# Forgetting attention: the softmax weights become the stationary operand of the weighted values

## The chip, the cores and the metric

The kernel runs on one core of a Trainium2 chip. The metric is the device time of the whole program in microseconds (us), taken over several runs; lower is better. The profile is of one execution. The engines are called as the profile calls them: PE (TensorE, matrix products), PEld (its loads of the stationary operand), DVE (VectorE), ACT (ScalarE), POOL (GpSimd) and SP, which issues most DMAs.

## What is computed

A trunk of two layers over 512 tokens of 1024 features. Layer 0 is causal softmax attention with 16 heads of 64 features and a forgetting bias; layer 1 is a gated linear recurrence (HGRN2). Each is followed by a gated MLP with a short causal convolution. The change touches only layer 0:

```python
def fox_mixer(h, w_in, b_f, w_out):
    q, k, v, fl = jnp.split(h @ w_in, [D, 2 * D, 3 * D], axis=-1)
    c = jnp.cumsum(jax.nn.log_sigmoid(fl + b_f), axis=1)
    ...
    logits = jnp.einsum('bhqd,bhkd->bhqk', qi, k) * scale
    logits = logits + (cqi[..., :, None] - c[:, :, None, :])
    logits = jnp.where(s_pos[None, :] <= t_pos[:, None], logits, -jnp.inf)
    p = jax.nn.softmax(logits, axis=-1)
    o = jnp.einsum('bhqk,bhkd->bhqd', p, v)
    ...
    return o @ w_out
```

## The kernel before

All of it lives on one core. Every float32 operand of a large product is split into two float32r parts, high and low (`split`, lines 66 to 68: ACT copies the high part, DVE subtracts to get the low one), and a product is three matmuls: high by high, high by low, low by high (`mm3`, lines 81 to 84). A projection (`proj`, line 86) makes 128 features by 512 tokens from 8 blocks of rows, 24 matmuls in all; its weights come as one 512 KB DMA into a tile `raw` (two buffers).

Attention goes over 8 pairs of heads. Four Python generators are interleaved by `conduct` (line 141): `projections` (main) issues one block of a projection, three matmuls, per step; `operands` puts finished q and k into the operands QX, KX, QQ, KK by DMA and transposes v; `maxima` computes logits to find the row maxima (tiles `mxp`); `attend` computes the logits again, transposed, with keys on the partitions (tiles `lg`), takes the exponential, masks it on POOL and splits it into `ph` and `pl`. A yield of n leaves n steps to the projections. Pair n+1's operands reuse the buffers of pair n-1, so they are begun only when pair n-1 is done. A scheduler then moves instructions within each engine; the order below is what it made.

In `attend`, one pair's transposed weights stand in five tiles: a0 (head 0, keys 0 to 127, all 512 queries), a1 (head 0, key tiles 1 and 3), c (key tile 2 of both heads), b0 and b1 (head 1). `weigh` (lines 459 to 467) uses the values as the stationary operand: 64 columns of `vh` or `vl` beside 64 columns of ones or zeros, and streams the weights of 512, 384, 256 and 128 queries past them, three matmuls per key tile. The result has features on the partitions for one head, the sum of the weights on the other 64 partitions. `evacuate` (lines 472 to 475) copies both out; the reciprocal of the sums is made with a logarithm, an exponential and a Newton step (lines 498 to 503), and `split` makes `oh` and `ol`, the operands of the output projection.

PSUM has three banks `b` for projections, three banks `s` (`side`) for all that runs beside them (mxp, rp, vT, pv), and two banks `lg`. The output projection begins before the last pairs are done: `early` (line 99) takes five blocks of output features (three in `b`, one in `s`, one in `lg`) through pairs 0 to 5, and does pairs 6 and 7 at the end. After that the MLP follows.

Of the kernel before, what the change touches and what calls it, by code (L numbers as in the profile page):

```python
# [8 lines left out]
F32 = mybir.dt.float32  # L9
# [19 lines left out]
# gain columns: att norm, hgrn norm, ffn norms, final norm, output norm, lower-bound logits  # L29
G_ATT, G_HGRN, G_FFN, G_FIN, G_ON, G_LB = 0, 1, 2, 4, 5, 6  # L30
# t-range starts of the transposed logits of key tile j
OFF = (0, 512, 1024, 896)
# [3 lines left out]
def trunk(ctx, tc, xT, gains, convs, bf, wqkv, wf, wo, wup, wdn, wh, wi, who, out):  # L36
# [8 lines left out]
    def bank(name):  # L45
        """a bank for a projection"""
        return ps.tile([P, S], F32, tag="b", name=name)

    def side(name):
        """a bank for what runs beside the projections"""  # L50
        return ps.tile([P, S], F32, tag="s", name=name)
# [34 lines left out]
    def proj(ap, xh, xl, name, kb=NB, bank=bank):  # L86
        """[128 features, S tokens] = W^T x; one step is one block of rows of W"""
# [11 lines left out]
    def early(aps, xh, xl, name, *more):  # L99
        """projections begun while the last two blocks of operands are still to come: three, and one for each  # L100
        of more, a bank and when it is free, whose weights take the place of operands used up before"""
# [39 lines left out]
    def conduct(main, *sides):  # L141
        """main issues one block of rows of a projection per step; a side stream yields how many steps
        to leave to main, or what it waits for"""
# [26 lines left out]
    class Norm:  # L170
# [24 lines left out]
        def finish(self, load=True):  # L195
            """rstd of each token, on every partition"""
# [27 lines left out]
    # =============== layer 0: forgetting attention ===============  # L224
    oscope = ExitStack()
    opool = oscope.enter_context(tc.tile_pool(name="opool", bufs=1, side="right"))
    with tc.tile_pool(name="att", bufs=2, side="right") as ap_:
# [6 lines left out]
        # first projections, block by block as x comes in  # L234
# [45 lines left out]
        # masks and persistent operands  # L280
        st = []
        for i in range(4):
            # rows of KX: k, cumulated gates, ones; of QX: q, ones, maxima; the sums of products of the low parts
            # come from KK and QQ
            t = {n: ap_.tile([P, S], F32R, name=f"{n}{i}", bufs=1) for n in ("KX", "QX", "KK", "QQ")}
            for n in ("KX", "QX"):
                G.memset(t[n][64:68].bitcast(F32), 1.0)
            st.append(t)
# [5 lines left out]
        for i in range(2):  # L294
            vh = ap_.tile([P, NT, 192], F32R, name=f"vh{i}", bufs=1)
            vl = ap_.tile([P, NT, 192], F32R, name=f"vl{i}", bufs=1)
            G.memset(vh[:, :, 64:128].bitcast(F32), 1.0)
            G.memset(vl[:, :, 64:128].bitcast(F32), 0.0)
            vst.append((vh, vl))
# [3 lines left out]
        def forget():  # L303
            """-8 * cumsum(log sigmoid) as rows, in two parts"""
# [13 lines left out]
        # pairs of heads whose keys, values, maxima and outputs are there  # L318
# [25 lines left out]
        def values(hp, o):  # L344
            """values, tokens on the partitions"""
            v32 = tmp(f"v32_{hp}")
            V.tensor_mul(v32, o, rstd)
            vh, vl = vst[hp % 2]
# [4 lines left out]
            vhv = vh.rearrange("p i (e d) -> p i e d", d=64)[:, :, 0::2, :]  # L353
            vlv = vl.rearrange("p i (e d) -> p i e d", d=64)[:, :, 0::2, :]
# [23 lines left out]
        def operands():  # L378
            """the products go on as soon as what they overwrite has been used"""
# [15 lines left out]
        def maxima():  # L395
            """of the rows of the logits; their negatives as rows of an operand"""
# [30 lines left out]
        def attend():  # L427
            """transposed logits, exponentials, weighted values with their sums beside them"""
            for hp in range(8):
# [3 lines left out]
                vh, vl = vst[hp % 2]  # L433
                parts = {}

                def logits(key, *blocks):
                    """blocks: head, key tile, first column in the bank"""
# [15 lines left out]
                    ph = ap_.tile([P, S], F32R, tag="ph", name=f"ph_{nm}", bufs=3)  # L453
                    pl = ap_.tile([P, S], F32R, tag="pl", name=f"pl_{nm}", bufs=3)
# [4 lines left out]
                def weigh(o, e, js):  # L459
                    cs = slice(64 * e, 64 * e + P)  # L460
                    for j in js:
                        ph, pl, c = parts[e, j]
                        s_ = slice(c, c + S - P * j)
                        oo = o[:, j * P:]
                        PE.matmul(oo, vh[:, j, cs], ph[:, s_], start=j == 0, stop=False)
                        PE.matmul(oo, vl[:, j, cs], ph[:, s_], start=False, stop=False)
                        PE.matmul(oo, vh[:, j, cs], pl[:, s_], start=False, stop=j == 2)

                dn = ap_.tile([P, S], F32, tag="dn", name=f"dn_{hp}", bufs=1)
                o32 = ap_.tile([P, S], F32, tag="o32", name=f"o32_{hp}", bufs=1)  # L470

                def evacuate(o, e):
                    a, b = slice(64 * e, 64 * e + 64), slice(64 - 64 * e, 128 - 64 * e)
                    A.copy(dn[a], o[b])
                    A.copy(o32[a], o[a])
# [7 lines left out]
                oa = side(f"pv_{hp}_0")  # L483
                weigh(oa, 0, (0,))
                logits("b0", (1, 0, 0))
                yield 2
                weigh(oa, 0, (1, 3))
# [3 lines left out]
                weigh(oa, 0, (2,))  # L491
                evacuate(oa, 0)
# [387 lines left out]
```

## Time and profile before

| | |
|---|---|
| median of 3 runs | 1280.43 us (1279.92 to 1281.11) |
| span of the profiled execution | 1279.4 us |
| attention with its output projection's start | 44 to 252 us of the span |
| one pair of heads in the steady part | about 26 us |
| mean granted clock of TensorE | 0.996 of full speed |

The span runs from the first to the last instruction of the profiled execution, whose own time outside the span is not listed; the median of the runs is 1.0 us above the span. In a timeline row the first number is the start, the second the duration; matmuls are pipelined, so the cost of one is the distance from its start to the next one's start, which is less than its duration. A bracket names what ended the idle time before an instruction. Line numbers are those of the kernel above.

### The profile page before, as it was taken

The numbers are of one execution on the slowest core, as the hardware profiler recorded it, in microseconds if no ns is written. First come the engines' busy times: TensorE is split into PE (matmuls) and PEld (weight loads), VectorE is DVE, ScalarE is ACT, GpSimd is POOL, SyncE is SP. The second block draws the span as 40 slices with busy tenths as digits, with TensorE's granted clock in tenths as the row PEclk, the third lists the DMA queues.
The fourth block names the chain that finished last, engine by engine and source line by source line (L and its number), as shares of the span: only waits on it lengthen the run. The fifth ranks groups of instructions, "written<-read, shape, count | busy, mean of one in ns | idle before, by whom it ended". The sixth has DMA issues, their size and how long they took to land.

```text
span 1279.4 us, 15645 instructions
## 1 busy us (share of the span) xinstructions
PE 1258.4 (98%) x5994; PEld 1042.7 (81%) x5994; DVE 803.0 (63%) x1235; ACT 589.8 (46%) x827; POOL 40.4 (3%) x110
## 2 busy tenths in 40 slices
PE   7999999999999999999999999999999999999997
PEld 5778888888888888888888888888888888888886
DVE  6767767387777777333367585566777777762233
ACT  6355556454444444222267565455544444442231
POOL 2011110000000000000100000000000000000001
PEclk9999999999999999999999999999999999999998
DMA  6544554233233333333322222222333333333321
GB/s 200 153 119 106 135 135 122 98 120 98 97 99 99 99 99 95 91 91 91 98 96 66 83 66 83 83 67 82 99 99 99 92 94 95 98 91 91 94 88 66
DMA packets 43306, 127.25 MB, mean 99 GB/s; under 512 B 5616, under 2 KB 8304, under 8 KB 43232
## 3 DMA queue, kind: packets, MB, share of 16 engines
q1 hardware_dynamic: 42592, 125.56, 32.6%
q8 instruction: 47, 0.77, 0.2%
q10 hardware_dynamic: 544, 0.52, 0.1%
q14 instruction: 27, 0.22, 0.1%
q0 software_dynamic: 96, 0.18, 0.1%
HBM read 111.43 MB, written 2.10 MB: 89 GB/s over the span
## 4 chain that ended last, share of the span: by engine, by line
PE 95%; DVE 2%; DMA 1%; ACT 1%; issue 0%; SPq 0%; POOL 0%; DVEq 0%; ACTq 0%
PE pj_up L82 12%; PE pj_up L84 12%; PE pj_up L83 12%; PE pj_dn L84 6%; PE pj_dn L82 6%; PE pj_dn L83 6%; PE i L629 1%; PE i L628 1%; PE i L626 1%; PE pj_who L83 1%; PE pj_wo L82 1%; PE pj_wo L83 1%; PE pj_who L84 1%; PE pj_who L82 1%; PE pj_wo L84 1%; PE pj_hf L82 1%
## 5 line engine op out<-in xcount | busy, mean ns | idle before, releaser
L84 PE MATMUL pj_up<-xh_f,wl_up 128*128 128x512 f32 x704 | 274.3, 390 | 0.0
L83 PE MATMUL pj_up<-xl_f,wh_up 128*128 128x512 f32 x704 | 274.3, 390 | 0.0
L82 PE MATMUL pj_up<-xh_f,wh_up 128*128 128x512 f32 x704 | 274.3, 390 | 0.0
L84 PEld LDWEIGHTS pj_up<-xh_f,wl_up 128*128 128x128 f32 x704 | 132.3, 188 | 27.5
L83 PEld LDWEIGHTS pj_up<-xl_f,wh_up 128*128 128x128 f32 x704 | 132.3, 188 | 27.3
L82 PEld LDWEIGHTS pj_up<-xh_f,wh_up 128*128 128x128 f32 x704 | 132.3, 188 | 27.2
L82 PE MATMUL pj_dn<-gh,wh_dn 128*128 128x512 f32 x330 | 131.0, 397 | 0.0
L84 PE MATMUL pj_dn<-gh,wl_dn 128*128 128x512 f32 x330 | 131.0, 397 | 0.0
L83 PE MATMUL pj_dn<-gl,wh_dn 128*128 128x512 f32 x330 | 131.0, 397 | 0.0
L67 ACT CAST wh_up<-raw_up 128x1024 fp32r<-128x1024 f32 x88 | 92.7, 1053 | 65.9 <-PE pj_up L83 51.5
L68 DVE TENSOR_TENSOR wl_up<-raw_up,wh_up 128x1024 fp32r<-128x1024 f32 x88 | 107.8, 1225 | 15.4 <-ACT wh_up L67 11.7
L68 DVE TENSOR_TENSOR wl_dn<-raw_dn,wh_dn 128x1024 fp32r<-128x1024 f32 (+1 forms) x45 | 51.1, 1136 | 97.9 <-ACT wh_dn L67 97.7
L543 DVE TENSOR_TENSOR us<-pj_up,rstd_f 128x512 f32<-128x512 f32 x88 | 60.6, 689 | 78.7 <-PE pj_up L84 78.6
L67 ACT CAST wh_dn<-raw_dn 128x1024 fp32r<-128x1024 f32 (+1 forms) x45 | 44.1, 980 | 140.4 <-PE pj_dn L83 114.0
L67 ACT CAST gh<-y 128x512 fp32r<-128x512 f32 x44 | 27.3, 620 | 115.5 <-DVE y L551 115.5
L546 ACT ACTIVATE y<-us,cv 128x512 f32<-128x512 f32 x88 | 71.7, 815 | 8.4 <-DVE us L543 7.3
L84 PEld LDWEIGHTS pj_dn<-gh,wl_dn 128*128 128x128 f32 x330 | 62.3, 189 | 15.0
L83 PEld LDWEIGHTS pj_dn<-gl,wh_dn 128*128 128x128 f32 x330 | 62.3, 189 | 15.0
L82 PEld LDWEIGHTS pj_dn<-gh,wh_dn 128*128 128x128 f32 x330 | 62.3, 189 | 15.0
L548 DVE SCALAR_TENSOR_TENSOR y<-us,cv,y 128x512 f32<-128x512 f32 x88 | 66.1, 752 | 3.0
L547 DVE SCALAR_TENSOR_TENSOR y<-us,cv,y 128x512 f32<-128x512 f32 x88 | 65.6, 745 | 0.2
L550 ACT ACTIVATE y<-y 128x512 f32<-128x512 f32 x44 | 27.8, 632 | 79.4 <-DVE y L548 79.4
(368 smaller groups left out, 2375.5 us busy)
## 6 DMA issues: line engine op xcount, KB each, us to landing
raw_up<-in_wup SPq DMA_DIRECT2D x88, 512.0 KB
raw_dn<-in_wdn SPq DMA_DIRECT2D x30, 512.0 KB
raw_dn<-in_wdn SPq DMA_DIRECT2D x15, 384.0 KB
raw_v<-in_wqkv SPq DMA_DIRECT2D x8, 512.0 KB
raw_wo<-in_wo SPq DMA_DIRECT2D x8, 512.0 KB
raw_hf<-in_wh SPq DMA_DIRECT2D x8, 512.0 KB
raw_hq<-in_wh SPq DMA_DIRECT2D x8, 512.0 KB
raw_hg<-in_wh SPq DMA_DIRECT2D x8, 512.0 KB
```

What stands on the lines that cost most here:

```text
L67: A.copy(dst_h, src)
L68: V.tensor_tensor(dst_l, src, dst_h.bitcast(F32), op=ALU.subtract)
L82: PE.matmul(o, wh_, xh_, start=first, stop=False)
L83: PE.matmul(o, wh_, xl_, start=False, stop=False)
L84: PE.matmul(o, wl_, xh_, start=False, stop=last)
L543: V.tensor_mul(u[:, 2:], o, rstd)
L546: A.activation(y, u[:, 2:], AF.Identity, scale=k(2), bias=k(3))
L547: V.scalar_tensor_tensor(y, u[:, 1:S + 1], k(1), y, op0=ALU.mult, op1=ALU.add)
L548: V.scalar_tensor_tensor(y, u[:, 0:S], k(0), y, op0=ALU.mult, op1=ALU.add)
L550: A.activation(ys[0], ys[0], AF.Silu)
L626: PE.matmul(o, xh[kk][:, ts_], hs, start=kk == 0 and i % 2 == 0, stop=False, skip_group_check=True)
L628: PE.matmul(o, xh[kk][:, ts_], ls, start=False, stop=False, skip_group_check=True)
```

## The change

For each tile of 128 queries, the transposed weights (128 keys by 128 queries of `ph`, then of `pl`) are now the stationary operand. Past `ph` stream 130 columns of one tile `v`: 64 of the low part of the values, 64 of the high part, 2 of ones; past `pl` stream the last 66 of them (`VW` is 130). The result has queries on the partitions, and the sums of the weights in a column beside it. So a reciprocal of 128 by 2 replaces the logarithm and exponential, `scale` multiplies and adds the two parts, and four transposes on PE bring the result back to features on the partitions. All five tiles of weights must be there before the third of the four query tiles, so `ph` and `pl` have five buffers instead of three, and all logits of a pair are issued ahead of all its weighted values. A pair's yields are now 28 steps instead of 21. Comments and docstrings went as well.

```diff
-            vh = ap_.tile([P, NT, 192], F32R, name=f"vh{i}", bufs=1)
-            vl = ap_.tile([P, NT, 192], F32R, name=f"vl{i}", bufs=1)
-            G.memset(vh[:, :, 64:128].bitcast(F32), 1.0)
-            G.memset(vl[:, :, 64:128].bitcast(F32), 0.0)
-            vst.append((vh, vl))
+            t = ap_.tile([P, NT, 2, VW], F32R, name=f"v{i}", bufs=1)
+            G.memset(t[:, :, :, 128:].bitcast(F32), 1.0)
+            vst.append(t)
...
-                    ph = ap_.tile([P, S], F32R, tag="ph", name=f"ph_{nm}", bufs=3)
-                    pl = ap_.tile([P, S], F32R, tag="pl", name=f"pl_{nm}", bufs=3)
+                    ph = ap_.tile([P, S], F32R, tag="ph", name=f"ph_{nm}", bufs=5)
+                    pl = ap_.tile([P, S], F32R, tag="pl", name=f"pl_{nm}", bufs=5)
...
-                def weigh(o, e, js):
-                    cs = slice(64 * e, 64 * e + P)
-                    for j in js:
-                        ph, pl, c = parts[e, j]
-                        s_ = slice(c, c + S - P * j)
-                        oo = o[:, j * P:]
-                        PE.matmul(oo, vh[:, j, cs], ph[:, s_], start=j == 0, stop=False)
-                        PE.matmul(oo, vl[:, j, cs], ph[:, s_], start=False, stop=False)
-                        PE.matmul(oo, vh[:, j, cs], pl[:, s_], start=False, stop=j == 2)
-                def evacuate(o, e):
-                    a, b = slice(64 * e, 64 * e + 64), slice(64 - 64 * e, 128 - 64 * e)
-                    A.copy(dn[a], o[b])
-                    A.copy(o32[a], o[a])
+                def weigh(i):
+                    o = side(f"pv_{hp}_{i}")
+                    for e in range(2):
+                        ov = o[:, e * VW:(e + 1) * VW]
+                        for j in range(i + 1):
+                            ph, pl, c = parts[e, j]
+                            s_ = slice(c + (i - j) * P, c + (i - j + 1) * P)
+                            PE.matmul(ov, ph[:, s_], v[:, j, e], start=e == 0 and j == 0, stop=False,
+                                      skip_group_check=True)
+                            PE.matmul(ov[:, 64:], pl[:, s_], v[:, j, e, 64:], start=False, stop=j == i,
+                                      skip_group_check=True)
+                    return o
+                def scale(o, i):
+                    ov = o[:, :2 * VW].rearrange("p (e d) -> p e d", d=VW)
+                    rc = ap_.tile([P, 2, 1], F32, tag="rc", name=f"rc_{hp}_{i}", bufs=2)
+                    V.reciprocal(rc, ov[:, :, 128:129])
+                    lo = ap_.tile([P, P], F32, tag="olo", name=f"olo_{hp}_{i}", bufs=2)
+                    on = ap_.tile([P, P], F32, tag="on", name=f"on_{hp}_{i}", bufs=4)
+                    for e in range(2):
+                        c = slice(64 * e, 64 * e + 64)
+                        A.activation(lo[:, c], ov[:, e, 0:64], AF.Copy, scale=rc[:, e])
+                        V.scalar_tensor_tensor(on[:, c], ov[:, e, 64:128], rc[:, e], lo[:, c],
+                                               op0=ALU.mult, op1=ALU.add)
+                    return on
...
-                oa = side(f"pv_{hp}_0")
-                weigh(oa, 0, (0,))
                 logits("b0", (1, 0, 0))
-                yield 2
-                weigh(oa, 0, (1, 3))
+                yield 3
                 logits("b1", (1, 1, 0), (1, 3, 384))
                 done["logits"] += 1
                 yield 3
-                weigh(oa, 0, (2,))
-                evacuate(oa, 0)
-                ob = side(f"pv_{hp}_1")
-                weigh(ob, 1, (0,))
-                yield 2
-                weigh(ob, 1, (1, 3, 2))
-                evacuate(ob, 1)
-                rc = tmp(f"rc_{hp}")
-                A.activation(rc, dn, AF.Ln)
-                A.activation(rc, rc, AF.Exp, scale=-1.0)
-                V.tensor_mul(dn, dn, rc)
-                V.scalar_tensor_tensor(rc, dn, 2.0, rc, op0=ALU.subtract, op1=ALU.mult, reverse0=True)
-                V.tensor_mul(o32, o32, rc)
+                ons = []
+                for i in range(NT):
+                    ons.append(scale(weigh(i), i))
+                    yield 2
+                tp = side(f"oT_{hp}")
+                for i in range(NT):
+                    PE.transpose(tp[:, i * P:(i + 1) * P], ons[i], ident)
...
-                split(oh[hp], ol[hp], o32)
+                A.copy(oh[hp], tp)
+                V.tensor_tensor(ol[hp], tp, oh[hp].bitcast(F32), op=ALU.subtract)
```

`values` writes the two parts of v into the halves of the new tile. Everything else is the same.

In PE's queue, third pair of heads (the second number in a name counts pairs from 0), part of the weighted values, before:

```order
L465 MATMUL pv_2_0_1079<-ph_2_a1_1044,vh0_344 128x384
L466 MATMUL pv_2_0_1079<-ph_2_a1_1044,vl0_345 128x384
L467 MATMUL pv_2_0_1079<-pl_2_a1_1045,vh0_344 128x384
L465 MATMUL pv_2_0_1079<-ph_2_a1_1044,vh0_344 128x128
L466 MATMUL pv_2_0_1079<-ph_2_a1_1044,vl0_345 128x128
L467 MATMUL pv_2_0_1079<-pl_2_a1_1045,vh0_344 128x128
L446 MATMUL lg_2_b1_1126<-QQ1_324,KK1_323 128x384
```

The same place after the change, the second of four query tiles:

```order
L467 MATMUL pv_2_1_1342<-v0_344,ph_2_a0_1165 128x130
L469 MATMUL pv_2_1_1342<-v0_344,pl_2_a0_1166 128x66
L467 MATMUL pv_2_1_1342<-v0_344,ph_2_a1_1224 128x130
L469 MATMUL pv_2_1_1342<-v0_344,pl_2_a1_1225 128x66
L467 MATMUL pv_2_1_1342<-v0_344,ph_2_b0_1281 128x130
L469 MATMUL pv_2_1_1342<-v0_344,pl_2_b0_1282 128x66
L467 MATMUL pv_2_1_1342<-v0_344,ph_2_b1_1303 128x130
L469 MATMUL pv_2_1_1342<-v0_344,pl_2_b1_1304 128x66
L82 MATMUL pj_k4_1307<-xh_a5_181,wh_k4_0_1310 128x512
```

Seven instructions that stream 384 or 128 columns became eight that stream 130 or 66, each with a stationary operand of its own; per pair there are 24 before and 40 now, and four transposes (`oT`).

In PE's queue, the last pair's first logits, before, with products of the output projection (`pj_wo`) among them:

```order
L84 MATMUL pj_wo1_2337<-oh1_976,wl_wo1_2341 128x512
L447 MATMUL lg_7_a0_2324<-QX2_328,KX2_327 128x512
L446 MATMUL lg_7_a1_2350<-QQ2_330,KK2_329 128x384
L447 MATMUL lg_7_a1_2350<-QX2_328,KX2_327 128x384
L446 MATMUL lg_7_a1_2350<-QQ2_330,KK2_329 128x128
L447 MATMUL lg_7_a1_2350<-QX2_328,KX2_327 128x128
L82 MATMUL pj_wo1_2337<-oh2_1208,wh_wo1_2340 128x512
L83 MATMUL pj_wo1_2337<-ol2_1209,wh_wo1_2340 128x512
L84 MATMUL pj_wo1_2337<-oh2_1208,wl_wo1_2341 128x512
L82 MATMUL pj_wo1_2337<-oh3_1474,wh_wo1_2340 128x512
```

After the change:

```order
L503 MATMUL oT_6_2692<-ident_68,on_6_2_2659 128x128
L444 MATMUL lg_7_a0_2701<-QQ2_330,KK2_329 128x512
L445 MATMUL lg_7_a0_2701<-QX2_328,KX2_327 128x512
L444 MATMUL lg_7_a1_2711<-QQ2_330,KK2_329 128x384
L445 MATMUL lg_7_a1_2711<-QX2_328,KX2_327 128x384
L444 MATMUL lg_7_a1_2711<-QQ2_330,KK2_329 128x128
L445 MATMUL lg_7_a1_2711<-QX2_328,KX2_327 128x128
L444 MATMUL lg_7_c_2724<-QQ2_330,KK2_329 128x256
L445 MATMUL lg_7_c_2724<-QX2_328,KX2_327 128x256
L444 MATMUL lg_7_c_2724<-QQ3_336,KK3_335 128x256
L445 MATMUL lg_7_c_2724<-QX3_334,KX3_333 128x256
L503 MATMUL oT_6_2692<-ident_68,on_6_3_2687 128x128
```

The projection products between the last pair's logits are gone: they stand ahead of this place now, beside the pair before it. From the last pair's first logits on PE has 57 fewer projection products left to issue than before.

## Rows read from the trace of the kernel before

**Rows 1.** The page's first part: busy us, share of span, instructions

```profile
PE 1258.4 (98%) x5994; PEld 1042.7 (81%) x5994; DVE 803.0 (63%) x1235; ACT 589.8 (46%) x827; POOL 40.4 (3%) x110
```

**Rows 2.** Windows: busy us by engine, granted clock, DMA share, GB/s

```profile
140.00:166.00 26.00, 25.71 (x128) 21.16 (x128) 18.41 (x40) 14.24 (x23) 3.15 (x8) 1.00 0.47 125
44.00:252.00 208.00, 204.87 (x1014) 168.71 (x1014) 137.84 (x290) 111.05 (x181) 23.95 (x64) 0.99 0.44 119
```

**Rows 3.** Waits of TensorE from 46 to 250 us: total us, times, longest

```profile
PE mxp L407 <- DMA KX<-kh: 2.0, 1, 2.0
PE mxp L407 <- DVE mx L409: 0.9, 4, 0.2
```

**Rows 4.** Timeline of TensorE, last head pair: start us, duration us, instruction

```profile
238.41 0.40 PE L465 MATMUL pv<-ph_b,vh 128*128 128x512 f32 x1
...
239.11 0.39 PE L82 MATMUL pj_wo<-oh,wxh_wo 128*128 128x512 f32 x1
...
240.51 0.34 PE L465 MATMUL pv<-ph_b,vh 128*128 128x384 f32 x1
...
241.03 0.22 PE L465 MATMUL pv<-ph_b,vh 128*128 128x128 f32 x1
241.09 0.28 PE L466 MATMUL pv<-ph_b,vl 128*128 128x128 f32 x1
241.20 0.28 PE L467 MATMUL pv<-pl_b,vh 128*128 128x128 f32 x1
241.31 0.33 PE L465 MATMUL pv<-ph_c,vh 128*128 128x256 f32 x1
...
241.72 0.40 PE L82 MATMUL pj_wo<-oh,wxh_wo 128*128 128x512 f32 x1
```

**Rows 5.** Timeline of TensorE, second head pair, runs of four merged

```profile
91.44 0.40 PE L420 MATMUL rp<-identr,rr 128*4 128x128 f32 x4
91.68 0.45 PE L465 MATMUL pv<-ph_b,vh 128*128 128x512 f32 x1
...
92.44 0.60 PE L351 MATMUL vT<-ident,v 128*128 128x128 f32 x4
92.80 0.42 PE L465 MATMUL pv<-ph_b,vh 128*128 128x384 f32 x1
```

**Rows 6.** Groups by line and form, ScalarE and VectorE: busy us, mean ns

```profile
L732 ACT ACTIVATE Sm<-S,s 128x128 f32<-128x128 f32 x24 | 9.7, 403 | 41.2 <-DVE S L728 35.7 <-DVE S L730 5.5
...
L474 ACT COPY dn<-pv 64x512 f32<-64x512 f32 x16 | 9.3, 580 | 28.8 <-PE pv L467 28.8
...
L730 DVE SCALAR_TENSOR_TENSOR S<-S,s,S 128x128 f32<-128x128 f32 x16 | 5.6, 352 | 0.6
```

**Rows 7.** Timeline of VectorE, end of the first head pair

```profile
63.42 1.22 DVE L68 TENSOR_TENSOR wl_q<-raw_q,wh_q 128x1024 fp32r<-128x1024 f32 x1
```

**Rows 8.** Timeline of all engines around TensorE's longest wait

```profile
78.09 0.33 SPq L72 DMA_DIRECT2D raw_k<-in_wqkv  x1
...
78.68 0.48 SPq L339 DMA_DIRECT2D KX<-kh  x1
...
83.02 0.30 PEld L407 LDWEIGHTS mxp<-KX,QX 66*128 66x128 f32 x2 [2.43 <-DMA KX<-kh]
```

**Rows 9.** Windows behind that wait

```profile
83.00:86.00 3.00, 2.98 (x13) 2.37 (x14) 2.47 (x9) 0.00 (x0) 0.00 (x0) 0.82 0.53 115
86.00:89.00 3.00, 3.00 (x12) 2.57 (x12) 1.78 (x7) 2.11 (x3) 0.00 (x0) 0.61 0.00 0
```

**Rows 10.** Timeline of ScalarE, last head pair's first two banks of weights

```profile
226.88 0.60 ACT L449 ACTIVATE pt_a<-lg_a 128x512 f32<-128x512 f32 x1 [1.81 <-PE lg_a L447]
227.87 0.62 ACT L67 CAST ph_a<-pt_a 128x512 fp32r<-128x512 f32 x1 [0.39 <-POOL pt_a L451]
228.40 0.59 ACT L449 ACTIVATE pt_a<-lg_a 128x512 f32<-128x512 f32 x1
229.65 0.62 ACT L67 CAST ph_a<-pt_a 128x512 fp32r<-128x512 f32 x1 [0.66 <-POOL pt_a L451]
```

More of the change, by code (lines that the diff above doesn't have):

```diff
@@ L30 @@
 G_ATT, G_HGRN, G_FFN, G_FIN, G_ON, G_LB = 0, 1, 2, 4, 5, 6
-OFF = (0, 512, 1024, 896)
+VW = 130
 @with_exitstack
@@ L347, in values @@
             V.tensor_mul(v32, o, rstd)
-            vh, vl = vst[hp % 2]
+            v = vst[hp % 2]
             tp = side(f"vT_{hp}")
@@ L352, in values @@
             tpv = tp.rearrange("p (i e d) -> p i e d", e=2, d=64)
-            vhv = vh.rearrange("p i (e d) -> p i e d", d=64)[:, :, 0::2, :]
-            vlv = vl.rearrange("p i (e d) -> p i e d", d=64)[:, :, 0::2, :]
+            vhv, vlv = v[:, :, :, 64:128], v[:, :, :, 0:64]
             A.copy(vhv, tpv)
@@ L432, in attend @@
                 tt = [st[2 * (hp % 2)], st[2 * (hp % 2) + 1]]
-                vh, vl = vst[hp % 2]
+                v = vst[hp % 2]
                 parts = {}
@@ L469, in attend @@
-                dn = ap_.tile([P, S], F32, tag="dn", name=f"dn_{hp}", bufs=1)
-                o32 = ap_.tile([P, S], F32, tag="o32", name=f"o32_{hp}", bufs=1)
-                def evacuate(o, e):
-                    a, b = slice(64 * e, 64 * e + 64), slice(64 - 64 * e, 128 - 64 * e)
-                    A.copy(dn[a], o[b])
-                    A.copy(o32[a], o[a])
+                def weigh(i):
[10 more added lines that the diff above has]
+                    return o
```

## The prediction

> **What bounds the kernel now.** I read the page's first part first: PE is busy for 98% of the span [rows 1], so a microsecond taken from or given to PE's queue is one of the whole time, and another engine counts only where PE waits for it. Next the windows: in the steady part of attention PE is busy for 25.71 of 26 us, while ACT has 14.24 and DVE 18.41 [rows 2]. Then the waits: between 46 and 250 us PE waits once for 2.0 us, for the DMA that brings the third pair's keys, and 0.9 us in four pieces for the row maxima on DVE [rows 3]; the granted clock there is 0.99 [rows 2]. So attention is a full PE queue with one hole, and the question is what the new queue costs, and how many holes it has.
>
> The timeline gives the price of a matmul as the distance of starts. For head 1 of the last pair the weighted values cost 239.11 - 238.41 = 0.70 us for the three of 512 columns, and 241.72 - 240.51 = 1.21 us for the three of 384, three of 128 and three of 256 [rows 4]: 1.91 us a head, 3.82 us a pair. The reader is to look at the three of 128 columns. The first is followed after 0.06 us, the other two after 0.11 us each [rows 4]. Four products that stream the same 128 columns past a stationary of only 4 columns take 91.68 - 91.44 = 0.24 us, 0.06 each [rows 5]. Same stream, another stationary: so in a run of short products it is the loading of 128 new columns that sets 0.11 us, and the stream does not. The first of a run is cheap because its load was done beside the long one ahead of it, and the long one behind the run pays it back.
>
> **The change part by part.**
>
> *Weighted values and transposes.* Removed: 24 products a pair, 3.82 us. Added: 40 products of 130 or 66 columns and four transposes, each with 128 new columns to load. At 0.11 us each [rows 4] that is 44 x 0.11 = 4.84 us. Eight pairs: 8 x 1.02 = +8.2 us, all in PE's queue. The columns streamed are halved, but they were not what a short product costs. The trace shows no long run of loads of this form, so bounds: four transposes, also with 128 new columns each, take 0.36 us, 0.09 each [rows 5], which gives 3.96 us a pair and +1.1 us in all; the run of 256 columns takes 0.41/3 = 0.137 us each [rows 4], which gives +17.7. I take 0.11, from the row with the nearest shape.
>
> The Trainium skill ("TensorE: Matmul & The Clock Gate", section "Back-to-back issue gap") gives for a sustained stream of weight load and matmul pairs about 81 ns each at 128 columns. By it the 44 would be 3.56 us and the change -2.1 us on PE instead of +8.2. This trace has 0.11 us in the middle of such a run [rows 4], so I don't follow it, but it is the price in a rival below.
>
> *ScalarE and VectorE.* A pair loses four copies of 0.58 us [rows 6], two passes for the reciprocal, and three passes on DVE. It gains eight ACT operations of 64 columns (0.40 us for 128 columns [rows 6], between half and all of that), eight on DVE (0.35 for 128 [rows 6], likewise) and four reciprocals. Both sums stay near what they were, and both engines have 7 us or more to spare of 26 [rows 2]: cost nothing, hidden beside the projections. What that cover does not hide is latency, since PE now reads their results back in the transposes. One `scale` is a reciprocal, two ACT operations, and a DVE operation behind the last: I estimate 0.2 + 2 x 0.3 + 0.25 = 1.05 us, 1.2 with the last product's own end. In the steady pairs six projection products, at 0.70/3 = 0.23 us [rows 4], and three transposes lie between (6 x 0.23 + 0.33 = 1.7 us): no wait. Removing the logarithm changes nothing else. The x tiles are no longer loaded into the place of the last `rc`, so their DMAs can start earlier: worth nothing, PE did not wait for them.
>
> *First pair.* Its four query tiles stand almost back to back in the new order, and each needs a bank `s`: the second waits for the bank that the cast of the maxima frees, the fourth for the one that `scale` of the first frees. In DVE's queue a split of projection weights of 1.22 us [rows 7] stands ahead of each. If PE paid for both whole, 2.4 us; if they fit, nothing. Stepping through it I get about 1.0 us.
>
> *The hole at the third pair.* Now PE waits 1.99 us for KX [rows 8], and the windows behind it show the granted clock at 0.82 and 0.61 [rows 9], the lower level (1.2 GHz) for part of each: (0.18 + 0.39) x 3 = 1.7 us of work lost. The hole costs 3.7 us. The keys were issued 0.6 us behind a 512 KB load of weights, 78.68 against 78.09, and came 4.3 us later [rows 8]. In the new order PE has 1.5 us less work between the end of that pair's k projection and the first maxima (15 projection products either way, beside them 1.0 us of logits instead of 2.5 us of logits and values), but the load ahead in SP's queue waits only for a split that lies some 5 us earlier, so it should be over. I estimate a wait of 1.2 us at full clock: 2.5 us won. Bounds: all 3.7 won, or 1.5 lost (3.5 us of wait and the slow stretch again).
>
> *The fourth pair.* It had no such wait. Now its k operand is made behind the second pair's last split on DVE, a chain of up to 7.2 us from the last transpose (copy, subtraction, k scaled, copy, 2.9 us in all, then up to 4.3 us of DMA [rows 8]), with about 5.5 us of products on PE beside it. Between 0 and 3.4 us (1.7, and 1.7 for the clock); I take 1.0. Behind the waiting mxp stand the projections, so nothing fills the hole.
>
> *Waits for maxima and transposes elsewhere.* The eight mxp of a pair stand closer together, with fewer products between. They cost 0.9 us before [rows 3]; I allow 0.8 us more, between 0 and 2.
>
> *Last pair.* The queue is 57 projection products (13 us) poorer from its first logits on. There ACT sets the pace: exponential and split of one bank are 226.88 to 228.40, 1.5 us [rows 10]. PE waits for the two `lg` banks to come free (about 0.9 us over three places), and for the last split of b0 (0.2). At the end six products (1.4 us) stand between the last weighted value and the transposes; then oh7 (0.6 us) must be copied before the 15 last products can go on, and nothing is left to put there: 1.2 us. I take 2.5 us, between 1 and 5. Before, the same stretch had no wait at all.
>
> *Sum.* 8.2 + 1.0 - 2.5 + 1.0 + 0.8 + 2.5 = +11.0 us. The profiled span of 1279.4 becomes 1290.4; the median stood 1.0 above the span, so the median of 1280.4 becomes 1291.4 us.
>
> **The rivals.**
>
> *More holes.* The terms for waits are small because PE's stops are short. If two of them reach the length of today's hole, each brings a slow stretch (1.7 us), and the tail costs 6 instead of 2.5. Then 11.0 + 3.4 + 3.5 = +17.9: 1298 us. For it: the chains from PE through DVE, ACT, DVE and back to PE are new, eight times four. Against it: they are short, and most have projections beside them.
>
> *Loads hidden in part.* If a run of loads goes at 0.09 us as the transposes do [rows 5], PE pays +1.1 instead of 8.2, and with the waits +2.8 it is +3.9: 1284.3 us. Against it: the merged row of four does not show where the load behind the fourth is paid, while the run of short products does [rows 4]. By the skill's 81 ns, named above, the time would be -2.1 + 2.8: 1281.1 us.
>
> *The stream decides: faster.* If 128 columns of stationary could be loaded beside the products as under the 4-column row, a pair of 130 and 66 columns costs 196/128 x 0.06 = 0.09 us, twenty of them 1.84, with transposes 2.2 us a pair instead of 3.82: -13 us. With +2.8 for waits, 1270 us. It decides once a load costs under 0.079 us, where 44 x 8 loads and the 2.8 us of waits equal the 30.6 us removed. Against it stands 0.11 in the run [rows 4], measured with the same shapes of load.
>
> *It doesn't do what it says.* The order shows 40 products and four transposes in every pair, so I give this nothing.
>
> **How the numbers follow.** My forecast, 1287 to 1297 us around 1291: 72%. More holes, 1297 to 1305: 15%. Loads hidden in part, 1281 to 1287: 7%. The stream decides: 3%. Anything else, mostly above 1302: 3%. The range 1284 to 1302 leaves out the last two, half of the third and a part of the second. A difference within 0.2% (2.6 us) is what a measurement of this kernel can't tell from none: faster than 1277.9 has 4%, within 4% (the cheap end of the hidden loads), slower 92%.
>
> **What would show it.** In the timeline after, starts of the products of 130 and 66 columns lie 0.11 us apart whatever their width; the weighted values with transposes take about 4.8 us of PE a pair, with PE's busy share of attention lower than now. The waits name `on` (from L482) at a transpose, `oh7` at the output projection, and KX at the third and fourth pair, each about a microsecond. The windows behind the third pair's maxima have a granted clock near 1. It is wrong if 66 columns cost clearly less than 130, if the steady pairs take less than 26 us of PE for their work, or if a wait of several microseconds stands where I have one.

## The result and the profile after

The kernel after takes 1296.46 us (median of 4 runs, 1295.26 to 1297.33) against 1280.77 us for the kernel before beside it: 1.0126 times as long, interval 1.0112 to 1.0140, or 15.7 us. The forecast was 1291.4 us, 1284 to 1302. The profiled execution spans 1294.0 us, 14.6 more than before. Nearly all of that lies in attention: from the first projection behind the start-up (33.09 us before, 32.72 after) to the first sum of the next norm (277.39 and 291.23) the two differ by 14.2 us, and what stands behind it by 0.8.

Three views of the kernel after answer to [rows 1 to 3]. The page's first part:

```profile
PE 1271.1 (98%) x6154; PEld 1053.8 (81%) x6154; DVE 805.4 (62%) x1307; ACT 583.2 (45%) x843; POOL 38.9 (3%) x108
```

The steady stretch among the windows:

```profile
142.00:168.00 26.00, 25.98 (x148) 22.00 (x146) 17.19 (x35) 13.05 (x24) 2.95 (x7) 1.00 0.49 124
```

And the waits of TensorE from 46 to 275 us, in total, times, longest:

```profile
PE oT L503 <- DVE on L482: 1.4, 3, 0.8
PE mxp L405 <- DVE v L354: 1.2, 1, 1.2
PE pj_wo L82 <- ACT oh L506: 0.7, 1, 0.7
PE pj_wo L82 <- ACT pt_b L447: 0.5, 1, 0.5
PE pv L467 <- DVE rrow L420: 0.3, 1, 0.3
PE pv L467 <- DVE v L354: 0.3, 1, 0.3
```

Over the whole span PE is as full as it was; it has 160 instructions more. The wait for KX, the longest of before, is gone, and in its place stand shorter ones for results of DVE or ACT, the longest of 1.2 us.

The price of the new products shows in a run of twelve in the second pair. The timeline's columns are start, duration, instruction:

```profile
98.06 0.22 PE L467 MATMUL pv<-v,ph_a 128*128 128x130 f32 x1
98.12 0.25 PE L469 MATMUL pv<-v,pl_a 128*128 128x66 f32 x1
98.20 0.31 PE L467 MATMUL pv<-v,ph_a 128*128 128x130 f32 x1
98.34 0.25 PE L469 MATMUL pv<-v,pl_a 128*128 128x66 f32 x1
98.42 0.31 PE L467 MATMUL pv<-v,ph_c 128*128 128x130 f32 x1
...
99.31 0.47 PE L82 MATMUL pj_k<-xh_a,wh_k 128*128 128x512 f32 x1
99.63 0.39 PE L83 MATMUL pj_k<-xl_a,wh_k 128*128 128x512 f32 x1
```

From the first short product to the second projection product are 1.57 us. Less the 0.23 us of one projection product, that is 1.34 us for twelve: 0.112 each. The first is cheap, 0.06, and the projection product behind the run pays it back, 0.32 instead of 0.23. Inside the run the spacing alternates, 0.14 behind 130 columns and 0.08 behind 66, 0.22 a pair.

What I had not forecast at all is in the windows over the first pair of the kernel after (the third value from the end is the granted clock, 1.00 for 2.4 GHz):

```profile
68.00:71.00 3.00, 2.70 (x24) 2.54 (x22) 2.31 (x8) 1.08 (x4) 0.00 (x0) 1.00 0.53 112
71.00:74.00 3.00, 3.00 (x14) 2.81 (x14) 1.26 (x6) 1.00 (x4) 0.00 (x0) 0.50 0.90 226
74.00:78.00 4.00, 4.00 (x12) 3.08 (x11) 0.83 (x2) 0.59 (x1) 0.00 (x0) 0.53 0.39 161
78.00:81.00 3.00, 3.00 (x15) 2.46 (x14) 2.28 (x3) 2.23 (x4) 0.85 (x1) 1.00 0.00 0
```

The timeline of TensorE where it falls:

```profile
70.71 0.25 PE L469 MATMUL pv<-v,pl_a 128*128 128x66 f32 x1
70.80 0.31 PE L467 MATMUL pv<-v,ph_b 128*128 128x130 f32 x1
70.94 0.32 PE L469 MATMUL pv<-v,pl_b 128*128 128x66 f32 x1
71.07 0.46 PE L467 MATMUL pv<-v,ph_b 128*128 128x130 f32 x1
71.33 0.36 PE L469 MATMUL pv<-v,pl_b 128*128 128x66 f32 x1
71.50 0.46 PE L467 MATMUL pv<-v,ph_c 128*128 128x130 f32 x1
```

The clock falls to its lower level (1.2 GHz) from 70.97 to 77.80 us in the middle of the first pair's weighted products, at a moment when PE is busy; the last wait that the trace names, of 0.28 us, ended at 68.39. The pair of short products goes from 0.22 to 0.43 us there (71.07 to 71.50). 6.83 us at half clock are 3.4 us of lost work. The fall lies in the longest run of its kind: from 67.03 to 72.83 us stand 36 weighted products and three transposes with no projection product between, while nowhere else in this kernel's attention do more than 19 stand in a row, and there the clock is full. The fall behind the third pair's maxima [rows 9] is gone.

### The profile page after: what moved, and what is told of

Its sections match the earlier page's. It is cut to its first block, busy times and chain, and to the rows that moved or that the text cites. A ratio compares the mean times of both kernels' runs of the same rounds, so it can differ in the third digit from the quotient of the medians.

```text
span 1294.0 us, 16074 instructions
## 1 busy us (share of the span) xinstructions
PE 1271.1 (98%) x6154; PEld 1053.8 (81%) x6154; DVE 805.4 (62%) x1307; ACT 583.2 (45%) x843; POOL 38.9 (3%) x108
## 4 chain that ended last, share of the span: by engine, by line
PE 88%; DVE 4%; issue 3%; ACT 2%; DMA 2%; POOL 1%; SPq 0%; DVEq 0%; ACTq 0%; POOLq 0%
PE pj_up L83 12%; PE pj_up L84 12%; PE pj_up L82 12%; PE pj_dn L82 6%; PE pj_dn L84 6%; PE pj_dn L83 6%; PE i L630 1%; PE i L629 1%; PE i L627 1%; PE pj_who L83 1%; PE pj_who L84 1%; PE pj_who L82 1%; PE pj_hf L82 1%; PE pj_hf L83 1%; PE pj_hf L84 1%
```

## The experiments

Each ran in five rounds beside the kernel before (1280.0 to 1281.6 us); ratios are to it, with the interval.

**Wide streams.** Is it the load or the columns?

```diff
-ov = o[:, e * VW:(e + 1) * VW]
+ov = o[:, 252 * e:252 * e + 260]
-PE.matmul(ov, ph[:, s_], v[:, j, e], ...)
-PE.matmul(ov[:, 64:], pl[:, s_], v[:, j, e, 64:], ...)
+PE.matmul(ov, ph[:, s_], vv[:, j], ...)   # both heads
+PE.matmul(ov, pl[:, s_], vv[:, j], ...)
```

`vv` is `v` with both heads' columns side by side; `scale` reads the result at its new columns.

> The kernel after, but every weighted product streams 260 columns (both heads of the pair; the columns of the other head land where nobody reads them) instead of 130 or 66. The loads of weights stay 320. Theory, a weighted product costs its load of 128 columns: its start spacing stays near the 0.11 us measured, at most the 0.12 us of the 256-column products of the kernel before, so at most 320 x 0.01 = 3 us more than the kernel after (1296.5), 1296 to 1300 us; less if the half clock in the first pair's weighted values (6.8 us of it in the kernel after) comes from the short streams. Rival, spacing follows the columns as the alternation of 0.14 us behind 130 columns and 0.08 us behind 66 suggests, about 0.02 + 0.00094 per column: 0.26 each at 260, 320 x 0.15 = 48 us more, about 1345 us.

1292.51 us, 1.0085 [1.0071, 1.0098]: with 2.65 times the columns it is 4 us *faster* than the kernel after. The timeline of its first pair:

```profile
70.02 0.28 PE L468 MATMUL pv<-v,ph_a 128*128 128x260 f32 x1
70.14 0.29 PE L470 MATMUL pv<-v,pl_a 128*128 128x260 f32 x1
70.27 0.28 PE L468 MATMUL pv<-v,ph_c 128*128 128x260 f32 x1
70.38 0.28 PE L470 MATMUL pv<-v,pl_c 128*128 128x260 f32 x1
...
71.22 0.39 PE L84 MATMUL pj_k<-xh_a,wl_k 128*128 128x512 f32 x1
```

0.12 us each, where 196 columns a pair gave 0.11: up to 260, the columns are nearly free. From start to start all weighted products take 39.3 us against 35.1. The alternation of 0.14 and 0.08 was thus no price of the columns. What makes the kernel faster lies elsewhere: PE's waits above 0.15 us fall from 5.9 to 2.2 us in attention, those for `on` among them, and the half clock is gone. Its windows, with the granted clock third from the end:

```profile
71.00:74.00 3.00, 3.00 (x26) 2.91 (x25) 1.44 (x7) 1.11 (x4) 0.00 (x0) 1.00 0.93 189
74.00:78.00 4.00, 4.00 (x19) 3.04 (x18) 1.86 (x4) 2.34 (x5) 0.30 (x1) 1.00 0.66 252
```

It stays at 1.00 through the stretch that ran at half in the kernel after.

**Wide streams in the first pair alone.**

```diff
-PE.matmul(ov, ph[:, s_], v[:, j, e], ...)
+PE.matmul(ov, ph[:, s_], vv[:, j] if hp == 0 else v[:, j, e], ...)   # pl likewise
```

> The kernel after, but only the first pair's 40 weighted products stream 260 columns. Theory, the half clock there (70.97 to 77.80 us, 3.4 us of work lost) comes from a run of short products with little else between: it goes, and the 40 products cost 0.01 us more each: 3.0 us less than the kernel after (1296.5), about 1293.5 us, of the 4.0 us that the wide streams gained in all pairs. Rival, the half clock comes from the waits of 0.34 and 0.28 us just before: it stays, 1296.5 to 1297 us, and the gain of the wide streams lay in the other pairs.

1293.60 us, 1.0096 [1.0081, 1.0111], 2.9 us under the kernel after, near the theory's 3.0, though the two intervals leave some 2.6 us either way; the trace has no half clock anywhere in attention. In the wide kernels the two short waits before the fall are gone too, so these two runs alone would not tell the streams from the waits. The kernel of the next paragraph speaks against the waits: its first pair has waits of the same kind (1.0 us in four pieces) and no fall. But it also has half as many short products, with four projection products among those from 66.88 us on, and in the wide kernels the new order puts projection products into the run as well (the one at 71.22 us above, for instance), so that no more than 19 products stand in a row. Whether the wider streams or the projections between kept the clock up is not shown.

**No products of the low parts, after and before.** Both kernels without the products of `pl`:

```diff
-PE.matmul(ov[:, 64:], pl[:, s_], v[:, j, e, 64:], ...)
```

> The kernel after without the 160 products of the low parts of the weights (the low part is left out of the values and of the sums). Theory, each product costs a load: 160 x 0.11 = 17.6 us less than the kernel after, about 1279 us. Rival, the 66 columns that stream set the cost, at the 0.23 us per 512 columns of the projections: 160 x 0.03 = 4.8 us less, about 1292 us. In between, the 0.08 us spacing seen behind 66 columns: 12.8 us less, about 1284 us.

1281.04 us, 1.0004 [0.9994, 1.0015]: 15.4 us less than the kernel after. The 160 products that stay take 17.8 us, 0.111 each, with 130 columns where the mean was 98. The waits of PE give some of it back:

```profile
PE oT L501 <- DVE on L480: 5.2, 5, 1.7
```

3.8 us more for `on` than in the kernel after, and half clock for 3.41 us instead of 6.83, 1.7 less: 15.4 + 3.8 - 1.7 = 17.5 us for 160 products, some 0.11 each. A load each, also by this road.

```diff
-PE.matmul(oo, vh[:, j, cs], pl[:, s_], ...)
```

> The kernel before without the 64 products of the low parts of the weights (the low part is left out of the values and of the sums), the same edit as in the kernel after without them, which gave 15.4 us for 160 products. Theory, with values stationary such a product costs its columns: 48 of 512, 384 and 256 columns at 0.23, 0.175 and 0.12 us and 16 of 128 at 0.11, so 16 x (0.23 + 0.175 + 0.12 + 0.11) = 10.2 us less than the kernel before, about 1270.6 us, so that the orientation of after pays 5 us more for the same part of the computation. Rival, a load each here too: 64 x 0.11 = 7.0 us less, about 1273.7 us.

1270.93 us, 0.9918 [0.9905, 0.9931]: 10.7 us less than before. That is near the 10.2 of its columns, but it is no clean price: the hole at KX is shorter (1.2 us), the half clock behind it is gone (1.7 us), a new wait of 0.9 us for the evacuation stands beside it, and maxima and projections start further apart. From start to start the weighted values take 21.7 us instead of 33.3: 11.6 less, off the 7.0 of its loads. Counted in this way, the same part of the computation costs 17.3 us in one orientation (35.1 to 17.8) and 11.6 in the other.

**The order of after with the orientation of before.** I wanted to split the price of the products from that of their order.

```diff
-tag="ph", bufs=3    # pl likewise
+tag="ph", bufs=5
-o32 = ap_.tile([P, S], F32, tag="o32", bufs=1)
+o32 = ap_.tile([P, S], F32, tag="pt", bufs=2)
-logits c, weigh a(0), logits b0, weigh a(1, 3), logits b1, weigh a(2), weigh b(0), weigh b(1, 3, 2)
+logits c, logits b0, logits b1, weigh a(0), weigh a(1, 3, 2), weigh b(0), weigh b(1, 3, 2)
```

The edit does more than its heading says: `o32`, the output before its division, takes one of the two buffers `pt` of the exponentials, and `mx` has one buffer instead of two.

> The kernel before (values are the stationary operand) in the order of the kernel after: five buffers of weights, all logits of a pair first, then the weighted values in steps. Theory, the loss is the price of the orientation on TensorE and what comes with it (waits of the transposes, half clock behind the short products): this kernel lands near the kernel before, 1278 to 1283 us, with the wait for KX at the third pair gone and the clock not halved in the first pair's weighted values. Rival, the order costs most: 1289 us or more, with the half clock in the first pair still there.

1296.96 us, 1.0120 [1.0104, 1.0135]. My theory fell: with the products of before, this edit costs as much as the whole change. But not in the way the rival had it, the clock in the first pair is full. The waits of PE from 235 us on:

```profile
PE pj_wo L82 <- ACT oh L67: 4.0, 1, 4.0
PE lg_c L446 <- ACT pt_a L449: 2.0, 1, 2.0
PE pv L465 <- ACT ph_a L67: 0.7, 2, 0.5
```

The long chain of ScalarE and VectorE passes for the reciprocal now stands behind the very last product, 10.24 and 6.83 us run at half clock (from 241.39 and 261.87), and PE waits 2.1 us, until 211.8 us, for the VectorE pass that scales a q projection. So I tried the order in seven pairs only:

```diff
+if hp < 7:  (order of after)
+else:       (order of before)
```

> The kernel before in the order of the kernel after for the first seven pairs, the last pair in the order of before. With the last pair in the new order too it took 1297.0 us, and its waits (2.0 us for the exponentials, 4.0 us for the last output) and 17 us at half clock all lay in the last pair. Theory, the order costs only there: 1279 to 1283 us, about the kernel before. Rival, the order costs in every pair: 1288 us or more.

1293.75 us, 1.0092 [1.0078, 1.0107]. The wait for the last output falls from 4.0 to 1.5 us and one of the two slow stretches goes, but the waits of 2.1 and 2.0 us stay, with the other slow one. So this theory, that the loss is the new order of the last pair, fell too, though most of the loss still lies in that pair (waits of 2.0 and 1.5 us, and 5.1 us for the slow stretch from 243.78). ScalarE's queue shows why the last pair still waits for its exponentials:

```profile
240.50 0.58 ACT L475 COPY dn<-pv 64x512 f32<-64x512 f32 x1 [2.84 <-PE pv L467]
...
241.71 0.63 ACT L527 ACTIVATE rc<-dn 128x512 f32<-128x512 f32 x1
242.36 0.60 ACT L449 ACTIVATE pt_a<-lg_a 128x512 f32<-128x512 f32 x1
...
244.90 0.60 ACT L449 ACTIVATE pt_a<-lg_a 128x512 f32<-128x512 f32 x1 [0.91 <-DVE pl_a L68]
```

The first exponential stands behind the two copies and the logarithm of the pair before, and the second waits for the split of the first (the other `pt` buffer holds `o32`, which is read until 248.5 us): they start 2.5 us apart, where [rows 10] had 1.5. PE has little to put there: from the last pair's first logits on 138 projection products are left in both kernels, where the kernel before had 177. So the two runs price the order together with the shared buffer, and what the order alone costs in the old orientation is not shown. They can't be subtracted from the kernel after; the price of the orientation rests on the four runs above.

**Later transposes.**

```diff
-yield 2
+yield 5 if i == NT - 1 and hp < 7 else 2
 tp = side(f"oT_{hp}")
```

> The kernel after, but in the first seven pairs the transposes of the outputs come 5 steps of the projections behind the last weighted products instead of 2. Theory, TensorE waits there for the chain reciprocal, low part, sum (1.4 us in 3 waits, 3.4 us of excess spacing over 0.11 each in all 32 transposes): 1.4 to 1.9 us less than the kernel after, about 1294.8 us, the half clock of the first pair unchanged. Rival, the transposes only collide with what follows (the maxima of the next pair) and the waits move there: 1296 to 1298 us.

1295.58 us, 1.0107 [1.0092, 1.0121]: its interval overlaps that of the kernel after, so no gain is shown, and the trace has three such waits again:

```profile
PE oT L503 <- DVE on L482: 1.6, 3, 0.8
```

A step is a turn of the projections, and it counts also when they have nothing to issue (their queue of three is full). At the longest of the three the transposes follow the last weighted product at once here too, with no projection in between. Nor is the distance the fault: ACT and DVE in the kernel after, at the longest of these waits:

```profile
216.25 0.17 DVE L476 RECIPROCAL rc<-pv 128x2 f32<-128x2 f32 x1
...
216.72 0.61 ACT L67 CAST wxh_wo<-raw_wo 128x512 fp32r<-128x512 f32 x1
...
217.06 0.68 DVE L346 TENSOR_TENSOR v<-pj_v,rstd_a 128x512 f32<-128x512 f32 x1
...
217.23 0.32 ACT L481 ACTIVATE olo<-pv,rc 128x64 f32<-128x64 f32 x1
...
217.65 0.68 DVE L68 TENSOR_TENSOR wxl_wo<-raw_wo,wxh_wo 128x512 fp32r<-128x512 f32 x1
...
218.25 0.28 DVE L482 SCALAR_TENSOR_TENSOR on<-pv,rc,olo 128x64 f32<-128x64 f32 x1
...
218.59 0.33 PE L503 MATMUL oT<-ident,on 128*128 128x128 f32 x1 [0.78 <-DVE on L482]
```

From the reciprocal to the end of `on` are 2.3 us, of which three passes of other work stand between (0.61 on ACT, twice 0.68 on DVE).

**The weighted values as early as their blocks allow.**

```diff
+logits a0, b0, a1; weigh tile 0; logits b1; weigh tile 1; logits c; weigh tiles 2, 3
-logits a0, a1, c, b0, b1; weigh tiles 0, 1, 2, 3
```

> The kernel after with the weighted values put in as soon as their blocks of weights exist (logits a0, b0, a1, weighted values of tile 0, b1, tile 1, c, tiles 2 and 3) instead of all logits first: 24 steps of a pair's path instead of 28, the same 320 products. Theory, the price of the loads (8.2 us) stays, and of the terms that belong to the order (waits for the transposed outputs and the values about 3 us, the last pair 2.3 us) some goes: 1293 to 1295 us, with the half clock of the first pair still there if its products still stand together. Rival, the order of after costs most of its 15.7 us: 1288 us or less. Second rival, the waits only move: 1296 to 1297 us.

1314.74 us, 1.0268 [1.0253, 1.0283]: 18 us worse, which neither theory had. The transposes no longer wait, but from the fourth pair on the maxima do:

```profile
PE mxp L405 <- DMA KX<-kh: 5.6, 2, 3.3
PE mxp L405 <- issue: 4.8, 3, 1.8
```

and six stretches of 3.41 or 6.83 us run at half clock. With the first pair wide as well:

```diff
+first pair's products 260 columns wide, as above
```

> As the one before, with the first pair's 40 products 260 columns wide. Theory, the two gains add (2.9 us for the first pair's clock): 1290 to 1292 us, still 9 us or more above the kernel before, since the loads stay. Rival, the clock did not fall in this order anyway: no difference to the one before it, or 0.4 us more.

1312.02 us, 1.0241 [1.0226, 1.0255], 2.7 us less, so most of the gain of the wide first pair may be there, but on a base 20 us higher than I had put it. Then the maxima later:

```diff
-yield 4
+yield 9 if hp >= 2 else 4
```

> The kernel with interleaved weighted values and a wide first pair (1312.0 us), with the maxima from the third pair on 9 steps of the projections behind the keys instead of 4 (3.4 us later). Theory, what the interleaved order lost are waits of the maxima for KX (five pairs, about 2.2 us each, 9.9 us) and the four half clocks behind them (8.5 us, of it the one at 237.19 and later ones in part without such a wait): most of it comes back, 1293 to 1298 us, about the kernel after, which its 28 steps a pair keep clear of that wait. Rival, the loss is the order of the weighted values itself: 1308 us or more.

1293.60 us, 1.0099 [1.0082, 1.0116]: 18.4 us come back with that one number. No wait for KX is left:

```profile
PE mxp L405 <- DVE on L484: 1.6, 5, 0.3
PE lg_b L444 <- ACT pt_b L447: 0.8, 1, 0.8
```

The wait of 0.8 us for an exponential lies in the first pair:

```profile
60.36 0.44 PE L444 MATMUL lg_b<-QQ,KK 128*128 128x384 f32 x1 [0.81 <-ACT pt_b L447]
```

Behind it the clock falls, from 61.50 to 68.33 us, with only four of the wide products in that stretch (the windows again):

```profile
61.00:64.00 3.00, 3.00 (x12) 2.47 (x13) 2.58 (x9) 1.95 (x4) 0.88 (x3) 0.58 0.12 45
```

In the run before this one it falls at 63.11 us, behind the same wait of 0.7 us. So a wide first pair does not keep the clock up in every order. The hole at KX, for its part, is set by how far the maxima stand behind the keys in PE's queue, and the order of the change, whatever else it costs, happens to keep clear of it.

**The hole in the kernel before.**

```diff
-yield 4
+yield 8 if hp == 2 else 4
```

> The kernel before, but the maxima of the third pair wait for 8 steps of the projections instead of 4. Theory of the hole: TensorE no longer waits 2.0 us for KX there and, having no wait before it, keeps its full clock: 3.7 us less than the kernel before (1280.8), about 1277 us. Rival, only the wait goes and the clock falls anyway: 2.0 us less, about 1278.8 us. Second rival, the wait comes back at another place: no change, 1280 to 1281 us.

1279.28 us, 0.9985 [0.9977, 0.9994]: 1.3 us, the one kernel of the same computation that beats both, by less than I call a difference. The trace has the mechanism:

```profile
PE mxp L407 <- DVE mx L409: 1.4, 5, 0.4
PE rp L420 <- DVE rr L415: 0.2, 1, 0.2
```

The wait for KX is gone and the windows from 83 to 89 us have a clock of 1.00, where [rows 9] had 0.82 and 0.61. From the end of the start-up to the next norm it takes 241.75 us (34.70 to 276.45) against 244.30: 2.55 of the 3.7 us, since PE waits 0.7 us more for maxima and their rows. The theory's 3.7 us was not reached; the rest of the difference to the 1.3 us of the medians is within what executions differ by (below).

## Why the prediction was right, and where its sum was off

The direction and the main mechanism held; the sum of +11.0 was 3.2 us under the +14.2 of attention. By its steps:

- *Price of the products, +8.2: right.* Measured 0.112 us in a run of twelve, and 0.11 by both accounts of the kernel without low products. 352 x 0.11 = 38.7, less 30.6. Over all of attention, with half clock and the waits above 0.15 us taken out, weighted products, transposes and the projections around them take 10.3 us more from start to start; 1.4 of it are gaps that stand under the fourth and the last pair below, which leaves 8.9. That 260 columns cost 0.12 shows that up to there the stationary sets it, as read from [rows 4, 5]. The rivals of loads partly hidden and of the stream that decides are out. The Trainium skill ("TensorE: Matmul & The Clock Gate", section "Back-to-back issue gap") gives about 81 ns for such a pair; by it, as an estimate, these loads would have cost 28.5 us. The trace, with 0.11 us each, does not agree. My sign, that starts would lie 0.11 apart whatever the width, was right only as a mean; by its letter the sign of being wrong came, 0.08 behind 66 columns and 0.14 behind 130, and only the wide streams showed that it meant nothing.
- *Hole at the third pair, -2.5: mis-sized, -3.7.* No wait is left. The reason was the right one: the loads of weights were issued nine microseconds ahead of the keys, so nothing stood before them, where [rows 8] had 0.6 us between the two:

```profile
71.12 0.58 SPq L72 DMA_DIRECT2D raw_v<-in_wqkv  x1
71.82 0.37 SPq L72 DMA_DIRECT2D raw_q<-in_wqkv  x1
80.41 0.48 SPq L338 DMA_DIRECT2D KX<-kh  x1
```

- *First pair, +1.0: 0.6 us of waits* (0.34 and 0.28). But what I left out is the step's real cost: I counted the dense run of its 40 products by waits alone, and thought of the clock only behind long waits. The half clock in it costs 3.4 us; the wide first pair gave 2.9 back. **This is the term that failed.**
- *Fourth pair, +1.0: 0.4 us*, and not for the reason given: its maxima begin at 109.99 us without a wait for KX. The 0.4 us are a gap of 0.60 instead of 0.23 between 110.63 and 111.23, where one of them waits for VectorE's maximum of another.
- *Waits for maxima and transposes elsewhere, +0.8: mis-sized, 1.7.* 1.4 us for `on` and 1.2 for `v`, with none instead of 0.9 for maxima (the 0.2 that is left is in the fourth pair's gap). I had priced the chain behind the last product as 1.2 us without what else stands in the queues of ACT and DVE; with it, it took 2.3. The one of 1.2 us came from further off: ACT waited 2.62 us for a load of output weights, and `olo`, the cast of `v` and the subtraction stood behind it.
- *Last pair, +2.5: 2.9 us* by the six longest gaps of PE's starts from 247.7 us on, less their usual spacing, among them 0.5 for an exponential and 0.7 for `oh`.

8.9 + 0.6 + 3.4 - 3.7 + 0.4 + 1.7 + 2.9 = 14.2 us. That the time lies inside the range owes something to luck: the hole, the waits of the first pair and the fourth came 2.2 us cheaper than forecast and hid part of the 3.4 us left out. The medians differ by 15.7, more than the two profiled spans: the profiled execution of after took 0.6 us less than its median, and that of before, by its span, about 0.3 us more (an execution here takes 1.7 to 1.8 us more than its span).

The rival of more holes gave 1298, nearer to the time than my sum, but it did not happen: no wait of after reaches 1.3 us, and the slow stretch had no long wait before it. That it could happen in this very orientation, the interleaved order shows.

## What to carry to other kernels

Count short products by the stationary operands they load, not by the columns they stream: here 130, 66 or 260 columns past 128 fresh ones all cost 0.11 to 0.12 us (512 cost 0.23), so an orientation that halves the columns and nearly doubles the loads loses. Look at the clock not only behind waits but also in dense runs of such products: here wider streams, with the order that came with them, brought 2.9 us back, and breaking up the run with projection products, which no run tried by itself, is the other thing to try. When an order is changed, ask at each DMA-fed operand how many microseconds of PE's queue stand between issue and use, since one number in that distance was worth 18 us here.

## What the runs showed of the hardware that I had not expected

- The granted clock fell to 0.50 in a run of 36 short products while PE was busy, its last wait 0.28 us long and 2.6 us earlier; with 260 columns a product, and projection products in the run, it stayed at 1.00. Waits before a fall were no reliable sign either: in the kernel before in the new order none followed the wait of 2.1 us at 211 us, and one followed that of 2.0 us at 240 us; in the last run of the interleaved order one followed a wait of 0.8 us.
- The start-up differs between executions: the first projection behind it came at 32.67 to 34.70 us in thirteen profiled executions, one of each kernel, a spread of 2.0 us that is larger than some of the effects above (33.09 and 34.70 in the kernel before and in the one with later maxima, which are the same up to there). Stretches of a trace are therefore compared from there, not from the span's start.
